# Start addresses of the tiles that TensorE reads as moving operands, and the sums of an RMSNorm by transposition, in a two-layer backbone on one core

## The chip, the cores and the metric

One core of a Trainium2 chip runs the whole program, alone. The metric is the device time of one execution in microseconds (us). A comparison is made of medians over several runs.

## What is computed

The reference runs two layers over 256 context tokens and 256 latent tokens of 1024 features, in float32:

```python
for l in range(DEPTH):                       # 2 layers
    m_lat = split(silu(c) @ w_ada[l] + b_ada[l], 9); m_ctx = the same of c_ctx
    x   = ffn_half(x,   m_lat[0:3], norm_g[l, 0], ffn_w1[l, 0], ffn_w2[l, 0])
    ctx = ffn_half(ctx, m_ctx[0:3], ...)
    h = modulate(rmsnorm(x, norm_g[l, 1]), m_lat[3], m_lat[4]) @ w_in[l]   # and of ctx
    y_lat, y_ctx = token_mixers(...)         # mLSTM, differential, neighbourhood attention
    x = x + m_lat[5] * y_lat
    x = ffn_half(x, m_lat[6:9], norm_g[l, 2], ffn_w1[l, 1], ffn_w2[l, 1])
    if l < DEPTH - 1: the same two steps for ctx
return rmsnorm(x, final_g)
```

`rmsnorm(x)` is `x / sqrt(mean(x*x) + 1e-6) * g`, the mean over the 1024 features of a token; `modulate(h)` is `h * (1 + scale) + shift`; `ffn_half` adds half of a gated `(silu(a) * b) @ w2`.

## The kernel before

All activations lie with features on the partitions and tokens along the free axis: `x` is 8 blocks of [128, 512 tokens], tokens 0 to 255 the context (class 0), 256 to 511 the latents (class 1).

A float32 product is made of three float32r matmuls. Each weight block (`raw`, by DMA) is split by ACT and DVE into `whi` and `wlo` (`weights`, `split`, L217 and L218), and each activation into a high and a low tile: `hhi`/`hlo` for a normed input or for the merged mixers (`split_pair`), `ghi`/`glo` for the gated hidden layer of an FFN (in the very first FFN the low part is two tiles, `head` and `tail`), `ohi`/`olo` for a mixer's output, `st`/`rest` for queries and keys. `three` (L230 to L232) then issues low x whi, high x whi, high x wlo: the weight block of 128x128 stands in the array, and the activation tile is the moving operand, read over 512 columns where both classes are wanted (`slice(0, T)`) or 256 for one class. In `v_part` (L632 to L634) the roles are swapped: a class's h blocks stand, and the weights move, 512 columns each.

The order of PE's instructions is written out by hand. Those of DVE, ACT and POOL are placed by a scheduler in the order of the code and its priorities (`tc.high_priority`). Small pieces of work are put in between the matmuls by `Beside`: a generator is stepped each time a counter of ticks passes given values, and a tick is one call of `three` (or three matmuls of `v_part`).

The norm before each stage is such a generator (`norm_mod`, `rstd_rows`, `rstd_cols`), one for each class. Its steps for a class are: two matmuls of `ssq` (the sums of squares by feature block, [128, 256]) with a column of ones, which leave the sum of each token in a column of PSUM (L260); on DVE the scaling by 1/1024 (L263); on POOL the power -0.5 (L264), giving `r`, [128, 2]; on DVE two diagonal matrices `dg` of it (L274); two matmuls of them with a matrix of ones, which lay the row of factors across all partitions (L278); then for each of 8 feature blocks `u` on DVE (L284), `hhi` on ACT (L286) and `hlo` on DVE (L287). The first step of a norm and its second are given by ticks: `beside.at(gen, (5, 12, 12, 12))` in `norm_begin` and in `ffn`, `(3, 6, 6, 6)` in `mixers`. Class 0's norm runs beside the last matmuls of the stage before, whose last pieces (`end(k)`) take one class, 256 columns, at a time; class 1's norm runs beside class 0's first matmuls of the new stage. The first FFN of the program has a start of its own (`cold_start`), so has the last (`warm_start`), which runs on latents alone, takes its first matmuls on x times the scale, and multiplies by `r` behind them. At the end, `rstd_cols` and a transposition of `x` give the output.

Of the kernel before, what the change touches and what calls it, by code (L numbers as in the profile page):

```python
# [10 lines left out]
F32 = mybir.dt.float32  # L11
F32R = mybir.dt.float32r
AF = mybir.ActivationFunctionType
ALU = mybir.AluOpType
# [97 lines left out]
def tile_backbone(ctx: ExitStack, tc: tile.TileContext, I, out: bass.AP):  # L112
# [27 lines left out]
    ones = cp.tile([P, P], F32, name="ones")  # L140
    nc.gpsimd.memset(ones, 1.0)
    half = cp.tile([P, 8], F32, name="half")
    nc.gpsimd.memset(half, -0.5)

    modT = [cp.tile([P, 9, 2, KC], F32, name=f"modT{l}") for l in range(L)]
# [91 lines left out]
            three(pt[:, at], w, slice(k * P, (k + 1) * P), a, (k0 + k, at), first and k == 0, last and k == n - 1)  # L237
            tick()

    def split_pair(name):  # L240
        return (hp.tile([P, KC, T], F32R, tag="hhi", name="hhi"),
                hp.tile([P, KC, T], F32R, tag="hlo", name="hlo"))


    ssq = cp.tile([P, T], F32, name="ssq")
# [9 lines left out]
    def rstd_cols(cs):  # L255

        n = (cs.stop - cs.start) // P
        p1 = psum()
        for t in range(n):
            mm(p1[:, t:t + 1], ssq[:, cs.start + t * P:cs.start + (t + 1) * P], ones[:, 0:1], start=True, stop=True)  # L260
        r = np_.tile([P, 4], F32, tag="r", name="r")
        with tc.high_priority(offset=AHEAD):
            nc.vector.tensor_scalar(r[:, :n], p1[:, :n], 1.0 / D, EPS, ALU.mult, ALU.add)  # L263
            nc.gpsimd.tensor_tensor(r[:, :n], r[:, :n], half[:, :n], ALU.pow)  # L264
        return r

    def rstd_rows(cs):

        n = (cs.stop - cs.start) // P
        r = rstd_cols(cs)  # L270
        dg = np_.tile([P, 2, P], F32, tag="dg", name="dg", bufs=1)
        with tc.high_priority(offset=AHEAD):
            for t in range(n):
                nc.vector.tensor_scalar_mul(dg[:, t, :], ident, r[:, t:t + 1])  # L274
        yield
        p2 = psum()
        for t in range(n):
            mm(p2[:, t * P:(t + 1) * P], ones, dg[:, t, :], start=True, stop=True)  # L278
        yield p2

    def norm_part(l, which, h, kc, cls, rb):
# [28 lines left out]
    def norm_begin(l, which, h, before):  # L310


        g, g1 = norm_mod(l, which, h, 0), norm_mod(l, which, h, 1)
        beside.at(g, (5, 12, 12, 12))
        for k in range(3):
            before(k)
        beside.drain(g)
        return g1
# [3 lines left out]
    def open_pool(name):  # L322
        e = stack["pool"] = ExitStack()
        return e.enter_context(tc.tile_pool(name=name, bufs=1, reuse_waits="tile"))
# [46 lines left out]
    def ffn(l, i, classes, out_classes_next, before, vectors):  # L371
# [9 lines left out]
        if both and before:  # L381
            gen = norm_begin(l, which, h, before)
        pool = open_pool(f"ff{l}{i}")
        ghi = pool.tile([P, NF, T], F32R, name="ghi")
        junk = pool.tile([P, 512], F32, name="junk") if both else None
        glo = Joined(pool, NF, 6) if cold else pool.tile([P, NF, T], F32R, name="glo")
# [63 lines left out]
        def warm_start():  # L450


            cls = classes[0]
            at = SLICES[1 - cls]
            ws = [w1_unit(k, soon=True, extra=pool if k else None) for k in range(2)]
            sh = pool.tile([P, KC, 32], F32, name="sh")
            nc.gpsimd.memset(sh, 0.0)
            nc.vector.tensor_copy(sh[:, :, 0], modT[l][:, 3 * which, cls, :])
            pts = [psum() for _ in range(2)]
            rows = rstd_rows(cs)  # L460
            for kc in range(KC):
                if kc == WARM[0]:
                    next(rows)
                elif kc == WARM[1]:
                    pr = next(rows)
                    with tc.high_priority(offset=AHEAD):
                        for k in range(KC):
                            norm_part(l, which, h, k, cls, pr[:, 0:256])
                    rb = np_.tile([P, 2, P], F32, tag="dg", name="rb", bufs=1).rearrange("p a t -> p (a t)")
                    nc.scalar.copy(rb, pr[:, 0:256])  # L470
                for pt, w in zip(pts, ws):
                    three(pt[:, cs], w, slice(kc * P, (kc + 1) * P), h, (kc, at), kc == 0, kc == KC - 1)

            pb = psum()
            for kc in range(KC):
                for g in range(4):
                    mm(pb[32 * g:32 * g + 32, 0:P], sh[:, kc, :], ws[g % 2][g // 2][:, kc * P:(kc + 1) * P].bitcast(F32),
                       start=kc == 0, stop=kc == KC - 1)
            lines = np_.tile([P, 256], F32, tag="rows", name="rows", bufs=1)[:, 0:P]
            with tc.high_priority(offset=AHEAD):  # L480
                nc.scalar.copy(lines, pb[:, 0:P])
            yield
            pT = psum()
            nc.tensor.transpose(pT[:, 0:P], lines, ident)
            bias = pool.tile([P, 2], F32, name="bias")
            nc.vector.tensor_reduce(out=bias, in_=pT[:, 0:P].rearrange("p (a m c) -> p m c a", a=2, m=2)[:, :, 0, :],
                                    axis=AX.X, op=ALU.add)
            ab = [pool.tile([P, 256], F32, name=name) for name in ("wa", "wb")]
            for k in range(2):
                nc.vector.tensor_tensor(ab[k], pts[k][:, cs], rb, ALU.mult)  # L490
                nc.scalar.activation(ab[k], ab[k], AF.Identity, bias=bias[:, k:k + 1])
            finish(0, *ab)

        if cold:
            cold_start(FIRST)
        elif not both:
            warm = warm_start()
            next(warm)
        elif both:

            ws = [w1_unit(k, extra=pool if k == 3 else None, soon=k < 2) for k in range(4)]
            pts = [psum() for _ in range(4)]
            beside.at(gen, (5, 12, 12, 12))
            for cls in (0, 1):
                if cls:
                    beside.drain(gen)
                at = SLICES[cls]
                for k in (0, 2):
                    for kc in range(KC):
                        for n in (k, k + 1):  # L510
                            three(pts[n][:, at], ws[n], slice(kc * P, (kc + 1) * P), h, (kc, at), kc == 0, kc == KC - 1)
                            tick()
                    if cls == 1:
                        act(k // 2, pts[k], pts[k + 1])
# [68 lines left out]
    def mixers(l, before):  # L583
# [7 lines left out]
        wf = I["wf"][l]  # L591
        wv = I["wv"][l]
        nlam = late["nlam"]
        h = split_pair("h")
        gen = norm_begin(l, 1, h, before)
        mp = open_pool(f"mx{l}")

# [6 lines left out]
        def loaded(name, shape, src):  # L604
            t = mp.tile(shape, F32, name=name)
            nc.scalar.dma_start(out=t, in_=src)
            return t
# [8 lines left out]
        cb = loaded("cb", [P, 2 * HML], I["conv_b"][l])  # L616
        mg = loaded("mg", [P, 4], I["ml_g"][l])
        dfg = loaded("dfg", [P, 4], I["df_g"][l])

        def proj(tile_i, cs):  # L620
            w = weights(wf[tile_i])
# [111 lines left out]
        pv1 = [psum() for _ in range(NT)]  # L733
        pg = psum()
        wv0, wv1 = weights(wv[0, 0], soon=True), weights(wv[0, 1], soon=True)
        beside.at(gen, (3, 6, 6, 6))
        wg = gate_weights()
        v_part(pv1, wv0, 0, (0, 1))
        v_part(pv1, wv1, 1, (0, 1))
# [416 lines left out]
        oT = [out_pair()]  # L1156
        na_out(oT[0])
        tgs.append(gate(2, 7, "t2k"))
        y = split_pair("y")
        for d2 in range(4):  # L1160
            branch(2, d2, oT[0], tgs[2 * d2:2 * d2 + 2], y)
        beside.drain()
# [192 lines left out]
```

## Time and profile before

| | us |
|---|---|
| median of 3 runs (lowest to highest) | 2288.07 (2287.82 to 2288.58) |
| the profiled execution, its own time | 2288.0 |
| its span, from the first instruction to the last | 2286.2 |
| busy: PE, its weight loads, DVE, ACT, POOL | 2253.8, 1948.1, 1580.5, 935.5, 81.3 |
| bytes read from HBM, over the span | 312.3 MB, 137 GB/s |

Two names are of use in reading it. The profile gives a matmul a start and a duration; the durations overlap, since one matmul enters the array while the one before it leaves, so what a stream of matmuls costs is read from one start to the next, not from the durations. And a matmul of float32 operands (not float32r) is shown as two records, a transposition as one: the two matmuls of L260 in a norm are four records.

### The profile page before, as it was taken

What the parts mean: (1) busy time and instruction counts of PE and PEld (TensorE: products, weight loads), DVE (VectorE), ACT (ScalarE), POOL (GpSimd) and SP (SyncE); (2) the same over time, 40 slices, a digit from 0 to 9 for tenths busy, and PEclk for the clock granted to TensorE, in tenths of its full rate; (3) what the DMA queues carried; (4) which work ended last, traced back from release to release, by engine and by line L of the source; (5) the groups of instructions that cost most, each with busy time, mean ns of one, the idle gap of its engine ahead of it and who ended that gap; (6) DMA issues with size and microseconds to landing.
All of it is one profiled execution on the core that took longest, in us unless ns stands there. A gap on an engine that the chain in (4) does not pass through costs nothing.

```text
span 2286.2 us, 33657 instructions
## 1 busy us (share of the span) xinstructions
PE 2253.8 (99%) x12845; PEld 1948.1 (85%) x12845; DVE 1580.5 (69%) x3398; ACT 935.5 (41%) x1687; POOL 81.3 (4%) x137
## 2 busy tenths in 40 slices
PE   7999999999999999999999999999999999999998
PEld 5888889888888788898888898888898898899998
DVE  5989944887665564676665479898248885768654
ACT  4323222455654553332322232322234675556443
POOL 0000000001002110000000000000000001200000
PEclk9999999999999999999999999999999999999999
DMA  8556543312222322334444436566323243445554
GB/s 302 179 199 203 192 136 97 102 65 74 74 84 85 92 83 83 111 116 147 161 151 144 138 111 205 201 202 197 100 95 115 70 137 122 138 145 169 184 178 136
DMA packets 94034, 315.55 MB, mean 138 GB/s; under 512 B 12928, under 2 KB 13712, under 8 KB 93872
## 3 DMA queue, kind: packets, MB, share of 16 engines
q1 hardware_dynamic: 89072, 308.07, 41.1%
q0 software_dynamic: 2144, 4.36, 1.4%
q8 instruction: 101, 1.65, 0.3%
q10 hardware_dynamic: 2656, 0.96, 0.2%
q14 instruction: 61, 0.50, 0.1%
HBM read 312.30 MB, written 1.05 MB: 137 GB/s over the span
## 4 chain that ended last, share of the span: by engine, by line
PE 87%; issue 9%; DVE 2%; DMA 1%; ACT 1%; POOL 0%; SPq 0%; POOLq 0%; DVEq 0%; ACTq 0%
PE p L230 25%; PE p L232 24%; PE p L231 24%; PE p L632 2%; PE p L634 2%; PE p L633 2%; PE p L657 1%; PE p L897 1%; PE p L1104 1%; DMA room<-in_w_ada 1%; PE p L952 1%; PE p L951 1%; PE p L1022 1%; PE p L874 1%; DVE wlo L218 0%
## 5 line engine op out<-in xcount | busy, mean ns | idle before, releaser
L230 PE MATMUL p<-hlo,whi 128*128 128x512 f32 (+1 forms) x2424 | 864.3, 357 | 2.7 <-DVE hlo L287 2.7
L232 PE MATMUL p<-hhi,wlo 128*128 128x512 f32 (+1 forms) x2424 | 848.5, 350 | 0.0
L231 PE MATMUL p<-hhi,whi 128*128 128x512 f32 (+1 forms) x2424 | 848.5, 350 | 0.0
L217 ACT CAST whi<-raw 128x1024 fp32r<-128x1024 f32 (+1 forms) x436 | 451.2, 1035 | 872.2 <-PE p L231 773.7
L218 DVE TENSOR_TENSOR wlo<-raw,whi 128x1024 fp32r<-128x1024 f32 (+1 forms) x436 | 524.0, 1202 | 292.2 <-ACT whi L217 291.2
L230 PEld LDWEIGHTS p<-hlo,whi 128*128 128x128 f32 x2424 | 459.8, 190 | 64.5 <-issue 3.7
L232 PEld LDWEIGHTS p<-hhi,wlo 128*128 128x128 f32 x2424 | 459.6, 190 | 59.8
L231 PEld LDWEIGHTS p<-hhi,whi 128*128 128x128 f32 x2424 | 459.9, 190 | 58.4 <-issue 1.9
L232 PE MATMUL p<-ghi,wlo 128*128 128x256 f32 (+1 forms) x836 | 278.2, 333 | 0.0
L231 PE MATMUL p<-ghi,whi 128*128 128x256 f32 (+1 forms) x836 | 276.7, 331 | 0.0
L196 DVE SCALAR_TENSOR_TENSOR junk<-raw,scb 128x512 f32<-128x512 f32 x256 | 176.1, 688 | 96.0 <-DMA raw<-in_w_adaT 95.5
L230 PE MATMUL p<-glo,whi 128*128 128x256 f32 (+1 forms) x616 | 203.1, 330 | 1.2 <-DVE x L305 1.2
L196 DVE SCALAR_TENSOR_TENSOR raw<-raw,scb 128x512 f32<-128x512 f32 x256 | 176.7, 690 | 6.1
L232 PEld LDWEIGHTS p<-ghi,wlo 128*128 128x128 f32 x836 | 156.9, 188 | 17.4
L231 PEld LDWEIGHTS p<-ghi,whi 128*128 128x128 f32 x836 | 156.8, 188 | 16.8
L230 PEld LDWEIGHTS p<-glo,whi 128*128 128x128 f32 x616 | 115.8, 188 | 11.5 <-DVE x L305 1.6
L305 DVE SCALAR_TENSOR_TENSOR x<-p,gmod,x 128x256 f32<-128x256 f32 x80 | 36.5, 480 | 83.6 <-PE p L232 83.3
L632 PE MATMUL p<-wlo,hhi 128*128 128x512 f32 x192 | 76.1, 396 | 0.0
L634 PE MATMUL p<-whi,hlo 128*128 128x512 f32 x192 | 74.9, 390 | 0.0
L633 PE MATMUL p<-whi,hhi 128*128 128x512 f32 x192 | 74.8, 390 | 0.0
L217 ACT CAST ghi<-g 128x512 fp32r<-128x512 f32 (+1 forms) x88 | 49.9, 567 | 58.2 <-DVE g L392 57.9
L230 PE MATMUL p<-olo,whi 128*128 128x512 f32 (+1 forms) x192 | 68.3, 356 | 0.0
(242 smaller groups left out, 2392.1 us busy)
## 6 DMA issues: line engine op xcount, KB each, us to landing
raw<-in_w SPq DMA_DIRECT2D x208, 512.0 KB, 3.4
raw<-in_w_adaT SPq DMA_DIRECT2D x128, 512.0 KB, 3.5
raw<-in_wf SPq DMA_DIRECT2D x106, 512.0 KB, 3.3
raw<-in_w SPq DMA_DIRECT2D x64, 448.0 KB, 3.3
raw<-in_wv SPq DMA_DIRECT2D x24, 512.0 KB, 3.2
raw<-in_wb SPq DMA_DIRECT2D x24, 512.0 KB, 3.3
room<-in_w_ada SPq DMA_DIRECT2D x16, 512.0 KB, 11.1
raw<-in_wo SPq DMA_DIRECT2D x16, 512.0 KB, 3.3
```

The lines of the kernel that those rows point to most:

```text
L196: nc.vector.scalar_tensor_tensor(w if cls else junk, w, 1.0, scb[:, cls, :], ALU.mult, ALU.mult, accum_out=acc[:, kc, i, cls:cls + 1])
L217: nc.scalar.copy(hi, src)
L218: nc.vector.tensor_sub(lo, src, hi.bitcast(F32))
L230: mm(dst, w[0][:, wat], a[1][:, aat[0], aat[1]], start=start, stop=False)
L231: mm(dst, w[0][:, wat], a[0][:, aat[0], aat[1]], start=False, stop=False)
L232: mm(dst, w[1][:, wat], a[0][:, aat[0], aat[1]], start=False, stop=stop)
L305: nc.vector.scalar_tensor_tensor(x[:, dt, cs], pt[:, cs], gmod[l][:, which, cls, dt:dt + 1], x[:, dt, cs], ALU.mult, ALU.add)
L632: mm(pts[t], h[0][:, kc, at], w[1][:, wat], start=kc == 0, stop=False)
L633: mm(pts[t], h[0][:, kc, at], w[0][:, wat], start=False, stop=False)
L634: mm(pts[t], h[1][:, kc, at], w[0][:, wat], start=False, stop=kc == KC - 1)
L657: nc.tensor.transpose(pt[:, k * P:(k + 1) * P], a, ident)
L874: mm(pS[:, rs], k[:, at], q[:, rs], start=True, stop=True)
```

## The change

It has three parts.

1. Padding is put ahead of some tiles (in `np_`, in the pools of the last FFN and of the mixers, and inside `hhi`/`hlo`, which become 32 elements longer), so that their start addresses in a partition move. The matmuls and their order stay. The table gives, for the float32r moving operands, the start address modulo 128 bytes in the two built programs; a read of class 1 starts 1024 bytes behind the tile's start, so it has the same remainder.

| moving tile | columns | reads | before | after |
|---|---|---|---|---|
| ghi, glo, head, tail | 512 | 1188 | 64 | 0 |
| ghi, glo, head, tail (FFNs of both classes) | 256 | 792 | 64 | 0 |
| ghi, glo (last FFN) | 256 | 528 | 64 | 64 |
| hhi, hlo | 512 | 4344 | 0 | 0 |
| hhi, hlo (layer 1's mixers, keys) | 512 | 288 | 0 | 64 |
| hhi, hlo (layer 1's mixers, last FFN) | 256 | 2240 | 0 | 64 |
| hhi, hlo (elsewhere) | 256 | 560 | 0 | 0 |
| ohi, olo | 512 | 288 | 32 | 0 |
| ohi, olo | 256 | 288 | 32 | 64 |
| st, rest (layer 0; layer 1) | 512 | 64; 64 | 32 | 0; 64 |
| st, rest | 256 | 64 | 32 | 0 |
| whi, wlo (as moving operands) | 512 | 576 | 0 | 0 |

2. The two matmuls with ones that sum `ssq` become two transpositions, and DVE sums the 128 columns of each (`tensor_reduce` over [128, 2, 128] in PSUM) ahead of the scaling. The two diagonal matrices and their matmuls become two transpositions of `r`, each column of it broadcast over 128 columns; the `dg` work on DVE is gone.

3. The ticks of a norm's second step go from 12 to 14 in the FFNs and at the end of each stage, and from 6 to 7 in the mixers.

```diff
-    def split_pair(name):
-        return (hp.tile([P, KC, T], F32R, tag="hhi", name="hhi"),
-                hp.tile([P, KC, T], F32R, tag="hlo", name="hlo"))
+    def split_pair(name, half_line=False):
+
+        at = 16 if half_line else 0
+        got = (hp.tile([P, KC * T + 32], F32R, tag="hhi", name="hhi"),
+               hp.tile([P, KC * T + 32], F32R, tag="hlo", name="hlo"))
+        return tuple(t[:, at:at + KC * T].rearrange("p (k t) -> p k t", k=KC) for t in got)
...
         for t in range(n):
-            mm(p1[:, t:t + 1], ssq[:, cs.start + t * P:cs.start + (t + 1) * P], ones[:, 0:1], start=True, stop=True)
+            nc.tensor.transpose(p1[:, t * P:(t + 1) * P], ssq[:, cs.start + t * P:cs.start + (t + 1) * P], ident)
         r = np_.tile([P, 4], F32, tag="r", name="r")
         with tc.high_priority(offset=AHEAD):
-            nc.vector.tensor_scalar(r[:, :n], p1[:, :n], 1.0 / D, EPS, ALU.mult, ALU.add)
+            nc.vector.tensor_reduce(out=r[:, :n], in_=p1[:, 0:n * P].rearrange("p (t c) -> p t c", t=n),
+                                    axis=AX.X, op=ALU.add)
+            nc.vector.tensor_scalar(r[:, :n], r[:, :n], 1.0 / D, EPS, ALU.mult, ALU.add)
             nc.gpsimd.tensor_tensor(r[:, :n], r[:, :n], half[:, :n], ALU.pow)
...
         r = rstd_cols(cs)
-        dg = np_.tile([P, 2, P], F32, tag="dg", name="dg", bufs=1)
-        with tc.high_priority(offset=AHEAD):
-            for t in range(n):
-                nc.vector.tensor_scalar_mul(dg[:, t, :], ident, r[:, t:t + 1])
         yield
         p2 = psum()
         for t in range(n):
-            mm(p2[:, t * P:(t + 1) * P], ones, dg[:, t, :], start=True, stop=True)
+            nc.tensor.transpose(p2[:, t * P:(t + 1) * P], r[:, t:t + 1].to_broadcast([P, P]), ident)
         yield p2
...
-        beside.at(g, (5, 12, 12, 12))
+        beside.at(g, (5, 14, 14, 14))
...
+        if not both:
+            pool.tile([P, 16], F32, name="half_line")
...
-        h = split_pair("h")
+        h = split_pair("h", not full)
...
+        mp.tile([P, 8 if full else 24], F32, name="line")
...
-        beside.at(gen, (3, 6, 6, 6))
+        beside.at(gen, (3, 7, 7, 7))
...
-        y = split_pair("y")
+        y = split_pair("y", not full)
```

Three places show how it moves instructions (line numbers of the changed kernel are a few higher). The first is PE at the end of layer 0's mixers, where class 0's norm for the next FFN lies between the matmuls of w_out. Before:

```order
L278 MATMUL p<-dg,ones 128x128 x2
L230 MATMUL p<-hlo,whi 128x256
L231 MATMUL p<-hhi,whi 128x256
L232 MATMUL p<-hhi,wlo 128x256
L230 MATMUL p<-hlo,whi 128x256
L231 MATMUL p<-hhi,whi 128x256
L232 MATMUL p<-hhi,wlo 128x256
```

and with the change, over the same stretch:

```order
L231 MATMUL p<-hlo,whi 128x256
L232 MATMUL p<-hhi,whi 128x256
L233 MATMUL p<-hhi,wlo 128x256
L231 MATMUL p<-hlo,whi 128x256
L232 MATMUL p<-hhi,whi 128x256
L233 MATMUL p<-hhi,wlo 128x256
L280 MATMUL p<-c_ident,r 128x128 x2
```

The second step of the norm stands two calls of `three` later, and is two transpositions (moving operand `c_ident`, the unit matrix).

The second place is DVE in the same norm (`x` is the residual sum of a block, `ssq` the running sum of squares, `wlo` the split of a weight block). Before:

```order
L263 TENSOR_SCALAR r<-p 128x2
L274 TENSOR_SCALAR dg<-c_ident,r 128x128 x2
L305 SCALAR_TENSOR_TENSOR x<-p,gmod_97,x 128x256
L218 TENSOR_TENSOR wlo<-raw,whi 128x1024
L284 SCALAR_TENSOR_TENSOR u<-x,amod_95,p 128x256 x3
L305 SCALAR_TENSOR_TENSOR x<-p,gmod_97,x 128x256
L253 TENSOR_TENSOR ssq<-ssq,sq 128x256
L218 TENSOR_TENSOR wlo<-raw,whi 128x1024
L253 TENSOR_TENSOR ssq<-ssq,sq 128x256
L305 SCALAR_TENSOR_TENSOR x<-p,gmod_97,x 128x256
L218 TENSOR_TENSOR wlo<-raw,whi 128x1024
L287 SCALAR_TENSOR_TENSOR hlo<-u,modT_93,hhi 128x256 x2
```

With the change:

```order
L267 TENSOR_REDUCE r<-p 128x2
L269 TENSOR_SCALAR r<-r 128x2
L307 SCALAR_TENSOR_TENSOR x<-p,gmod_98,x 128x256
L219 TENSOR_TENSOR wlo<-raw,whi 128x1024
L257 TENSOR_TENSOR ssq<-ssq,sq 128x256
L286 SCALAR_TENSOR_TENSOR u<-x,amod_96,p 128x256 x3
L307 SCALAR_TENSOR_TENSOR x<-p,gmod_98,x 128x256
L219 TENSOR_TENSOR wlo<-raw,whi 128x1024
L257 TENSOR_TENSOR ssq<-ssq,sq 128x256
L307 SCALAR_TENSOR_TENSOR x<-p,gmod_98,x 128x256
L219 TENSOR_TENSOR wlo<-raw,whi 128x1024
L289 SCALAR_TENSOR_TENSOR hlo<-u,modT_94,hhi 128x256 x2
```

The two `dg` rows are gone, a reduction is new, and the `ssq` of a block, which needs ACT's square of it, stands ahead of the three `u` instead of behind them.

The third place is DVE in class 1's norm at the start of layer 0's mixers. `mg` and `dfg` are small constants that come by DMA from ACT's queue, `nselr` the copy of another, `wg` the split of the gates' weights. Before:

```order
L274 TENSOR_SCALAR dg<-c_ident,r 128x128 x2
L287 SCALAR_TENSOR_TENSOR hlo<-u,modT_93,hhi 128x256 x2
L218 TENSOR_TENSOR wg<-raw,wg 128x8x8 x2
L284 SCALAR_TENSOR_TENSOR u<-x,amod_95,p 128x256 x3
L287 SCALAR_TENSOR_TENSOR hlo<-u,modT_93,hhi 128x256 x2
L284 SCALAR_TENSOR_TENSOR u<-x,amod_95,p 128x256
L287 SCALAR_TENSOR_TENSOR hlo<-u,modT_93,hhi 128x256
L284 SCALAR_TENSOR_TENSOR u<-x,amod_95,p 128x256 x2
L287 SCALAR_TENSOR_TENSOR hlo<-u,modT_93,hhi 128x256
L748 CAST nselr<-nsel 128x64
L814 TENSOR_SCALAR mg<-mg 128x4
```

With the change:

```order
L267 TENSOR_REDUCE r<-p 128x2
L289 SCALAR_TENSOR_TENSOR hlo<-u,modT_94,hhi 128x256
L269 TENSOR_SCALAR r<-r 128x2
L289 SCALAR_TENSOR_TENSOR hlo<-u,modT_94,hhi 128x256
L219 TENSOR_TENSOR wg<-raw,wg 128x8x8 x2
L286 SCALAR_TENSOR_TENSOR u<-x,amod_96,p 128x256 x3
L289 SCALAR_TENSOR_TENSOR hlo<-u,modT_94,hhi 128x256
L819 TENSOR_SCALAR mg<-mg 128x4
L820 TENSOR_SCALAR dfg<-dfg 128x4
L286 SCALAR_TENSOR_TENSOR u<-x,amod_96,p 128x256
L289 SCALAR_TENSOR_TENSOR hlo<-u,modT_94,hhi 128x256 x2
L286 SCALAR_TENSOR_TENSOR u<-x,amod_96,p 128x256
```

`mg` and `dfg` now stand behind the first `hlo` of class 1 instead of behind the fourth and the seventh, and `nselr` further back. The queue of ACT issues the same DMAs in the same order. Layer 1's mixers change alike.

## Rows read from the trace of the kernel before

**Rows 1.** The page, busy time: engine, busy us (share of the span), instructions.

```profile
PE 2253.8 (99%) x12845; PEld 1948.1 (85%) x12845; DVE 1580.5 (69%) x3398; ACT 935.5 (41%) x1687; POOL 81.3 (4%) x137
```

**Rows 2.** The page, costliest groups: busy us, mean ns, idle before and its releaser.

```profile
L217 ACT CAST whi<-raw 128x1024 fp32r<-128x1024 f32 (+1 forms) x436 | 451.2, 1035 | 872.2 <-PE p L231 773.7
```

**Rows 3.** Timeline of PE, 100 to 140 us: start us, duration us, instruction.

```profile
99.83 0.39 PE L230 MATMUL p<-hlo,whi 128*128 128x512 f32 x1
...
139.95 0.39 PE L230 MATMUL p<-hlo,whi 128*128 128x512 f32 x1
```

**Rows 4.** Timeline of PE, 310 to 350 us.

```profile
309.61 0.39 PE L230 MATMUL p<-head,whi 128*128 128x512 f32 x1
...
349.44 0.39 PE L230 MATMUL p<-tail,whi 128*128 128x512 f32 x1
```

**Rows 5.** Timeline of PE, 902 to 922 us.

```profile
902.13 0.39 PE L230 MATMUL p<-olo,whi 128*128 128x512 f32 x1
...
921.81 0.39 PE L230 MATMUL p<-olo,whi 128*128 128x512 f32 x1
```

**Rows 6.** Timeline of PE, 2100 to 2122 us.

```profile
2099.95 0.28 PE L230 MATMUL p<-hlo,whi 128*128 128x256 f32 x1
...
2121.91 0.28 PE L230 MATMUL p<-hlo,whi 128*128 128x256 f32 x1
```

**Rows 7.** Timeline of PE, 2220 to 2242 us.

```profile
2219.73 0.28 PE L230 MATMUL p<-glo,whi 128*128 128x256 f32 x1
...
2241.99 0.28 PE L230 MATMUL p<-glo,whi 128*128 128x256 f32 x1
```

**Rows 8.** Timeline of PE, 389.5 to 391 us.

```profile
389.98 0.28 PE L232 MATMUL p<-ghi,wlo 128*128 128x256 f32 x1
390.09 0.50 PE L260 MATMUL p<-ones,ssq 128*128 128x1 f32 x4
...
390.66 0.28 PE L231 MATMUL p<-ghi,whi 128*128 128x256 f32 x1
```

**Rows 9.** Timeline of PE, 600 to 601.5 us.

```profile
600.29 0.39 PE L232 MATMUL p<-hhi,wlo 128*128 128x512 f32 x1
600.52 0.38 PE L657 MATMUL p<-c_ident,de 128*128 128x128 f32 x2
...
600.98 0.40 PE L231 MATMUL p<-hhi,whi 128*128 128x512 f32 x1
...
601.45 0.40 PE L230 MATMUL p<-hlo,whi 128*128 128x512 f32 x1
```

**Rows 10.** Timeline of PE, 966 to 974 us.

```profile
968.53 0.28 PE L232 MATMUL p<-hhi,wlo 128*128 128x256 f32 x1
971.49 0.58 PE L230 MATMUL p<-hlo,whi 128*128 128x256 f32 x1 [2.67 <-DVE hlo L287]
```

**Rows 11.** Timeline of ACT, 960 to 985 us.

```profile
968.74 1.04 ACT L217 CAST whi<-raw 128x1024 fp32r<-128x1024 f32 x1 [1.51 <-PE p L231]
```

**Rows 12.** Stretches: busy us (instructions) of each engine, granted PE clock, DMA share, GB/s.

```profile
971.50:977.60 6.10, 6.10 (x28) 6.04 (x28) 3.67 (x12) 1.52 (x3) 0.70 (x1) 0.50 0.25 86
```

**Rows 13.** Timeline of ACT and its queue (ACTq), 392 to 420 us.

```profile
404.01 0.44 ACTq L606 DMA_DIRECT2D dfg<-in_df_g  x1
...
406.19 0.33 ACTq L606 DMA_DIRECT2D nsel<-in_nsel  x1
```

**Rows 14.** Timeline of DVE, 392 to 420 us.

```profile
406.06 0.88 DVE L287 SCALAR_TENSOR_TENSOR hlo<-u,modT,hhi 128x256 fp32r<-128x256 f32 x2
...
409.33 0.20 DVE L748 CAST nselr<-nsel 128x64 fp32r<-128x64 f32 x1 [0.43 <-DMA nsel<-in_nsel]
...
413.24 0.48 DVE L287 SCALAR_TENSOR_TENSOR hlo<-u,modT,hhi 128x256 fp32r<-128x256 f32 x1
```

**Rows 15.** Timeline of PE, 413 to 416 us.

```profile
415.16 0.28 PE L728 MATMUL p<-hlo,wg 128*128 128x256 f32 x1
```

**Rows 16.** Groups by form, DVE: the same columns as rows 2.

```profile
L1078 DVE TENSOR_REDUCE nmx<-p 128x1 f32<-128x256 f32 x16 | 6.2, 415 | 6.7 <-PE p L952 6.7
```

More of the change, by code (lines that the diff above doesn't have):

```diff
@@ L142, in tile_backbone @@
     half = cp.tile([P, 8], F32, name="half")
+    np_.tile([P, 16], F32, tag="line", name="line", bufs=1)
     nc.gpsimd.memset(half, -0.5)
@@ L468, in warm_start @@
                             norm_part(l, which, h, k, cls, pr[:, 0:256])
-                    rb = np_.tile([P, 2, P], F32, tag="dg", name="rb", bufs=1).rearrange("p a t -> p (a t)")
+                    rb = np_.tile([P, 256], F32, tag="dg", name="rb", bufs=1)
                     nc.scalar.copy(rb, pr[:, 0:256])
@@ L502, in ffn @@
             pts = [psum() for _ in range(4)]
-            beside.at(gen, (5, 12, 12, 12))
+            beside.at(gen, (5, 14, 14, 14))
             for cls in (0, 1):
```

## The prediction

> **What bounds the kernel now.** I read the busy times first: PE is busy for 99% of the span [rows 1], and the reader is to see that no other engine comes near. Then the groups: ACT's cast of a weight block, the head of the chain that feeds PE, sits idle for 872 us, 774 of them waiting for PE to give a weight buffer back [rows 2]. So weights are ready ahead of PE, and what PE saves on its own stream comes off the end, stage by stage, except where PE itself waits. Last I read PE's timeline, from start to start, since durations of matmuls overlap.
>
> That timeline, laid beside the start addresses of the change's table, shows three spacings for 512 columns. In the first FFN, hhi and hlo start at 0 modulo 128 bytes: 177 steps take 139.95 - 99.83 = 40.12 us, 226.7 ns each [rows 3]. head, tail and ghi start at 64: 174 steps in 39.83 us, 228.9 ns [rows 4]. olo and ohi start at 32: 84 steps in 19.68 us, 234.3 ns [rows 5]. For 256 columns the order turns round: at 0, 183 steps in 21.96 us, 120.0 ns [rows 6]; at 64, 189 steps in 22.26 us, 117.8 ns [rows 7]. All five stretches run without a gap. They differ in tiles and stages too, so the address is inferred; but tiles of other pools with the same remainder keep the same spacing (whi and wlo moving in the v products that of rows 3, glo in the later FFNs that of rows 4).
>
> **The addresses, term by term** (reads of the change's table times the difference of these spacings).
> - 512 columns from 64 to 0, 1188 reads x 2.24 ns: -2.7 us.
> - 512 columns from 32 to 0, 288 of ohi and olo and 64 of st and rest, x 7.6 ns: -2.7.
> - 512 columns from 32 to 64, 64 reads x 5.4: -0.3.
> - 512 columns from 0 to 64 (layer 1's keys), 288 x 2.24: +0.6.
> - 256 columns from 0 to 64, 2240 x 2.22: -5.0.
> - 256 columns from 64 to 0 (the FFNs of both classes, whose tiles serve both widths), 792 x 2.22: +1.8.
> - 256 columns from 32 to 64 or 0: no clean stretch shows them; between 117.8 and 120.0 on either side, 352 reads come to 0.8 us at most one way or the other, and I take 0.
>
> Sum -8.3 us. Bounds: if the address is not the cause, 0. On the other side, the reads of hhi and hlo at 0 are not always at 227 ns: behind a group of float32 matmuls they stand at 235, as the two steps from 600.98 to 601.45 do [rows 9]. I count 744 of the 4344 between 228 and 240 ns, most in layer 0's mixers. If they fell into step once no neighbour starts at 32, that would be 744 x 6 ns, a further -4.4. I take none of it, since the stretch of rows 9 comes from a transposition and not from a 32.
>
> **The norms on PE.** A pair of float32 matmuls is four records. From the matmul ahead of them to the second behind them is 390.66 - 389.98 = 0.68 us [rows 8]; without them it would be two spacings, 0.24, so the group costs 0.44. Two transpositions cost 600.98 - 600.29 = 0.69 less two spacings of 0.227, so 0.24 [rows 9]. A group that turns from the one into the other saves 0.21 us. There are 12 sums and 11 row spreads; without the cold start's four, where PE waits for weights anyway, and the last sum, which ends the program, 18 lie in PE's stream: -3.8 us.
>
> **The norms' chain.** On DVE the two dg products go, and with them a wait for POOL inside DVE's order; a reduction of 256 columns comes in, 415 ns by the attention's own [rows 16]. In the middle of the program the chain has room. The second step stands two ticks later, six matmuls of 0.12 us or 0.7 us, less 0.42 that PE saves by then, so the factors come 0.3 us later relative to PE (0.26 in the mixers, with one tick of 0.68). The shortest room I find where PE does not already wait is that of the last block of class 1 in the mixers: written by 413.24 + 0.48 = 413.72 [rows 14], read at 415.16 [rows 15], 1.4 us. It covers that. Cost 0; if the cover were gone, each tenth lost is a tenth of PE's.
>
> The moved mg and dfg are a new wait. nsel was usable 3.1 us after its issue (406.19 to 409.33) [rows 13, 14], so dfg, issued at 404.01, is usable at 407.1. DVE comes to it behind the first hlo of class 1, of the pair that begins at 406.06 [rows 14], so at about 406.5, and waits 0.6 us. Queued behind it are the other blocks' u and hlo, which PE needs in turn, and they have the 1.4 us or more. Cost 0, twice in the program.
>
> At the end nothing hides the chain: the reduction adds 0.4 us, PE's shorter sum gives 0.2 back: +0.2.
>
> **Where PE waits now.** At the start of layer 0's second FFN PE stops from 968.53 to 971.49 for the first hlo [rows 10]. ACT could make hhi only behind a cast that waits for the weight buffer which PE's last matmul gives back, at 968.74 [rows 11]; ACT's order there is not changed, and the whole wait moves with PE. Behind it PE's granted clock is 0.50, the 1.2 GHz level, for 6.1 us in which it is busy all the time [rows 12], so some 3 us are lost. I keep both. Late next, should a stall go, would be the third weight block's split.
>
> **Sum**: -8.3 - 3.8 + 0.2 = -11.9 us. The profiled execution took 2288.0, the median of the runs is 2288.07, the same; so 2276.1.
>
> **A rule against the change.** The rows say that 512 columns cost 226.7, 228.9 or 234.3 ns by where they start [rows 3 to 5]. The Trainium skill, "SBUF — State Buffer", in its specifications and its note on cachelines, has lines of 16 bytes and a penalty for leaving a line too early: starts at 0, 32 and 64 all begin a line and read the same number of whole lines, so by it the padding would give nothing. No run here shows lines of 16 bytes, and rows 3 to 7 speak against that being all there is.
>
> **Rivals.**
> 1. The address does not count; the spacings belong to the stages (their DMA traffic, their PSUM use) and stay. For it: no tile is read at two addresses with the same width in this trace. Against: one remainder, one spacing, across stages. It leaves -3.8 + 0.2: 2284.4, less than 0.2% from before. This is also what the page's rule comes to.
> 2. Only one width follows the address. 512 columns alone give -2.7 - 2.7 - 0.3 + 0.6 = -5.1, with the norms 2279.3; 256 alone give -5.0 + 1.8 = -3.2, so 2281.2.
> 3. More than the sum: the float32r reads of the mixers fall into step (-4.4, 2271.7), or the 0.50 stretch at 971 us does not come, since PE arrives there a few us earlier (-3, 2273.1); both, 2268.7.
> 4. Slower: a norm comes late. If class 0's first hlo missed PE at the start of both mixers and of layer 1's first FFN as it does at 971 us, each place would cost the wait of 2.67 and the half clock's 3.05 [rows 10, 12], 5.7 us, and three of them 17.1: 2288.0 - 11.9 + 17.1 = 2293.2. It decides where the factors come later than the room: over 1.4 us against the 0.3 (0.9 with the DMA) worked out above. ACT's order speaks for it a little, since in both mixers two casts now stand ahead of the first hhi.
>
> **How the numbers follow.** The sum, 2276.1, with a range of its own of 2273.5 to 2279.0, I give 0.68; rival 3 0.14; rival 2 0.08; rival 1 0.06; rival 4 0.04. About 0.2% (4.6 us) is what a measurement of this kernel can tell from no change. Faster by more: 0.68 + 0.14 + 0.08 = 0.90; within it 0.06; slower 0.04. The range leaves out rivals 1 and 4 and the ends of 2 and 3: 2269.5 to 2281.0.
>
> **What would show it.** In the profile after, 512 columns of ghi should stand at 226.7 ns and not 228.9, those of ohi near 227, and the last FFN's 256 columns of hhi at 117.8 and not 120.0, while 256 columns of ghi in FFNs of both classes rise to 120. A norm's two groups should each take 0.24 us and be two records. The wait of some 2.7 us at the start of layer 0's second FFN should stand where it did, with a half-clock stretch behind it. The prediction is wrong if those spacings stay as they are, or if PE shows new waits for hlo in the mixers.

## The result, and the profile after

The changed kernel takes **2303.0 us** (median of 4 runs, 2301.1 to 2304.2), the kernel before beside it 2287.95 (2286.4 to 2288.6): a ratio of 1.0065, 95% interval 1.0053 to 1.0076. It is **slower by 15 us, where 2276.1 was forecast**. The profiled execution took 2301.13 us, its span 2299.4, against 2288.0 and 2286.2.

The page's busy times and its group of the weight casts (busy us, mean ns, idle before and its releaser), to be laid beside [rows 1, 2]:

```profile
PE 2266.4 (99%) x12799; PEld 1935.7 (84%) x12799; DVE 1581.5 (69%) x3388; ACT 936.1 (41%) x1687; POOL 82.2 (4%) x137
L218 ACT CAST whi<-raw 128x1024 fp32r<-128x1024 f32 (+1 forms) x436 | 451.0, 1035 | 925.8 <-PE p L232 829.2
```

PE is still busy for 99% of the span, with 46 records fewer and 12.6 us more. The cast waits longer for PE than before. So weights do not come too late: PE's own stream has become slower.

The timeline of PE (start us, duration us, instruction), four stretches that answer to [rows 3 to 6]:

```profile
99.08 0.40 PE L231 MATMUL p<-hlo,whi 128*128 128x512 f32 x1
...
139.68 0.40 PE L231 MATMUL p<-hlo,whi 128*128 128x512 f32 x1
...
316.08 0.40 PE L231 MATMUL p<-tail,whi 128*128 128x512 f32 x1
...
349.68 0.40 PE L231 MATMUL p<-tail,whi 128*128 128x512 f32 x1
...
911.06 0.39 PE L231 MATMUL p<-olo,whi 128*128 128x512 f32 x1
...
929.43 0.39 PE L231 MATMUL p<-olo,whi 128*128 128x512 f32 x1
...
2108.76 0.28 PE L231 MATMUL p<-hlo,whi 128*128 128x256 f32 x1
...
2131.86 0.28 PE L231 MATMUL p<-hlo,whi 128*128 128x256 f32 x1
```

- hhi and hlo with 512 columns, whose remainder modulo 128 did not change: 174 steps in 40.60 us, **233.3 ns, for 226.7 before** [rows 3].
- tail and ghi, moved from 64 to 0: 144 steps in 33.60 us, **233.3 ns, for 228.9** [rows 4], where 226.7 was forecast.
- olo and ohi: 81 steps in 18.37 us, 226.8 ns, for 234.3 [rows 5], as forecast.
- hhi and hlo with 256 columns: 196 steps in 23.10 us, 117.9 ns, for 120.0 [rows 6], as forecast (one of the 196 is a transposition in between).

Two of the four go the wrong way, and they are the wide ones: 4632 and 1188 reads. The built program tells what they have in common. hhi starts where it did, but is 128 bytes longer, so hlo, the next tile, starts 128 bytes further on. Modulo 128 that is nothing. The tiles behind the two start 320 bytes further on: twice 128, and 64 for the padding in `np_`. **Modulo 256, hlo went from 0 to 128, and ghi, glo, head and tail from 64 to 128**; ohi and olo are at 0 (layer 0). In the kernel before, every tile that I had called "0" was at 0 modulo 256 as well.

Adding up PE's timeline from each start to the next by kind of instruction, against the profiled execution of before, gives the account below; the other columns are kernels of the next section. A wait of PE is counted with the instruction ahead of it. The cold start lies in two rows and nearly cancels: about -1.3 in the norms', +1.6 in the rest.

| us against before | the change | hlo mended (`e2`) | and g at 0 (`e5`) | layer 1's h at 112 (`e8`) |
|---|---|---|---|---|
| hhi, hlo, 512 columns, 4632 reads | +17.6 | +0.2 | -0.8 | -0.3 |
| ghi, glo, head, tail, 512 columns, 1188 | +4.5 | +5.2 | -2.7 | -2.7 |
| v products (whi, wlo moving), 576 | +3.3 | +2.8 | +2.7 | +2.8 |
| ohi, olo, 512 columns, 288 | -1.2 | -1.4 | -1.3 | -1.3 |
| 256 columns of h, g and o, 4408 | -6.6 | -4.7 | -6.0 | -12.1 |
| the norms' sums and row spreads | -6.4 | -6.3 | -6.7 | -6.4 |
| the rest (start, end, other matmuls) | +1.9 | +2.4 | +1.9 | +2.1 |
| sum | +13.1 | -1.8 | -12.9 | -17.9 |

The first row is less than 4632 times the 6.6 ns of the first FFN: over the 960 such reads of layer 0's second FFN the change stands at 231.1 ns, not 233.3 (226.7 before). Why the two differ is not shown.

### The profile page after: what moved, and what is told of

The parts are those of the page before. It is cut to its first block, busy times and chain, and to the rows that moved or that the text cites. A ratio compares the mean times of both kernels' runs of the same rounds, so it can differ in the third digit from the quotient of the medians.

```text
span 2299.4 us, 33562 instructions
## 1 busy us (share of the span) xinstructions
PE 2266.4 (99%) x12799; PEld 1935.7 (84%) x12799; DVE 1581.5 (69%) x3388; ACT 936.1 (41%) x1687; POOL 82.2 (4%) x137
## 4 chain that ended last, share of the span: by engine, by line
PE 86%; issue 9%; DVE 3%; DMA 1%; ACT 1%; SPq 0%; POOLq 0%; POOL 0%; DVEq 0%; ACTq 0%
PE p L231 25%; PE p L233 24%; PE p L232 24%; PE p L639 2%; PE p L638 2%; PE p L637 2%; PE p L662 1%; PE p L902 1%; PE p L1109 1%; DMA room<-in_w_ada 1%; PE p L957 1%; PE p L956 1%; PE p L1027 1%; PE p L879 1%; DVE wlo L219 1%
## 5 line engine op out<-in xcount | busy, mean ns | idle before, releaser
L233 PEld LDWEIGHTS p<-ghi,wlo 128*128 128x128 f32 x836 | 158.1, 189 | 17.6
L396 DVE TENSOR_TENSOR g<-g,p 128x512 f32<-128x512 f32 (+1 forms) x87 | 54.0, 621 | 29.9 <-PE p L233 29.4
```

The costliest lines, as they stand in the source:

```text
L233: mm(dst, w[1][:, wat], a[0][:, aat[0], aat[1]], start=False, stop=stop)
L396: nc.vector.tensor_tensor(g, g, b, ALU.mult)
```

## The experiments

After the result I held three theories. **A**: what counts is the moving tile's own start, but modulo 256. **B**: it is the distance between the start of the moving and that of the standing tile, or of the low and the high tile, which here looks like A because whi and wlo start at 0 modulo 256 nearly everywhere. **C**: the addresses have nothing to do with it, and the new norms or something at the start put the stream into another state.

**Mend one length.** `e2_line256`: the change, with hhi and hlo 64 elements longer in place of 32.

```diff
-        got = (hp.tile([P, KC * T + 32], F32R, tag="hhi", name="hhi"),
-               hp.tile([P, KC * T + 32], F32R, tag="hlo", name="hlo"))
+        got = (hp.tile([P, KC * T + 64], F32R, tag="hhi", name="hhi"),
+               hp.tile([P, KC * T + 64], F32R, tag="hlo", name="hlo"))
```

> The changed kernel with hhi and hlo 64 elements longer instead of 32, so that hlo starts at 0 (or 64) modulo 256 as hhi does, not at 128 (192); all other remainders stay. Theories A and B: hlo and hhi back at 226.7 ns, the v products too, so 17.6 and 3.3 us come off: 2303.0 - 20.9 = about 2282. Theory C: 2303.

Measured: 2283.8 us (10 runs), ratio 0.9985 (0.9975 to 0.9994). The same stretch of PE's timeline as above:

```profile
98.98 0.39 PE L231 MATMUL p<-hlo,whi 128*128 128x512 f32 x1
...
139.78 0.39 PE L231 MATMUL p<-hlo,whi 128*128 128x512 f32 x1
```

180 steps in 40.80 us, 226.7 ns again. 128 bytes in one tile's length are worth 19 us. C falls. The v products did not come back as expected (+2.8 in the account); `e5_g0` below shows why.

**One part of the change each.** `e3_norms` is the kernel before with the transpositions, the reduction and the new ticks; `e4_addr` is the change's padding with the norms and ticks of before.

```diff
# e3_norms, against the kernel before
-            mm(p1[:, t:t + 1], ssq[:, cs.start + t * P:cs.start + (t + 1) * P], ones[:, 0:1], start=True, stop=True)
+            nc.tensor.transpose(p1[:, t * P:(t + 1) * P], ssq[:, cs.start + t * P:cs.start + (t + 1) * P], ident)
...
# e4_addr, against the changed kernel
-            nc.tensor.transpose(p1[:, t * P:(t + 1) * P], ssq[:, cs.start + t * P:cs.start + (t + 1) * P], ident)
+            mm(p1[:, t:t + 1], ssq[:, cs.start + t * P:cs.start + (t + 1) * P], ones[:, 0:1], start=True, stop=True)
...
```

> The kernel before with the new norms and ticks alone, no address moved. Theories A and B: the norm groups' saving alone, 4 to 6 us: 2282 to 2284. Theory C, if the transpositions put the stream out of step: 2300 or more.

> The changed kernel with the norms and ticks of the kernel before: the addresses alone. Theories A and B: the changed kernel's time plus the norms' 4 to 6 us: 2307 to 2309. Theory C: about the kernel before, 2288.

Measured: the norms alone 2284.09 us, ratio 0.9985 (0.9975 to 0.9994), 3.4 us below the 2287.44 beside it. The padding alone 2307.06, ratio 1.0086 (1.0071 to 1.0101), 19.6 us above. The two parts are nearly additive: 19.6 - 3.4 = 16.2, for the 15 of the whole. The norms were forecast right, the padding with the wrong sign.

**The starts by themselves.** `e1_starts` runs triples (low moving tile over high standing, high over high, high over low), 16 in a row, at each pair of starts, at both widths.

```python
for w in STAND:            # standing tiles wa..wd start at 0, 64, 128, 192
    for m in MOVE:         # moving tiles la..lh (low), ha..hh (high) at 0, 32, ... 224
        seg512(m, w)
```

> This kernel leaves the whole network out: it runs streams of float32r triples (low x first block, high x first block, high x second block) alone, 48 matmuls for each pair of start addresses, and gives zeros and one block of PSUM back. The moving tiles start at 0, 32, ... 224 bytes past a multiple of 1024 (la/ha to lh/hh), the standing ones at 0, 64, 128, 192 (wa/va to wd/vd). Theory A (the moving operand's start modulo 256 bytes sets the spacing): 512 columns from 0 at 226.7 ns, from 64 and 192 at 229, from 32, 96, 160, 224 at 234, from 128 at 232 to 235, the same whatever the standing start is. Theory B (what counts is where moving and standing operands, or low and high tile, start relative to each other): moving 128 beside standing 128 is as fast as 0 beside 0, and equal low and high tiles are faster than low at 128 with high at 0. Theory C (not the addresses, but a state of the stream that something before it leaves behind): one spacing for all starts, and other values where the same starts come a second time.

Of its trace, by line and tile, the first matmul of each triple: duration ns min/median/max, first and last start us. From the first to the last are 15 triples.

```profile
L67 PE MATMUL p<-la,wa x16: 389/389/389, 26.9 to 37.1; 128*128 128x512 f32 x16
...
L67 PE MATMUL p<-lc,wa x16: 388/388/398, 49.0 to 59.3; 128*128 128x512 f32 x16
...
L67 PE MATMUL p<-le,wa x16: 392/394/398, 71.2 to 81.7; 128*128 128x512 f32 x16
...
L67 PE MATMUL p<-la,wb x16: 394/394/399, 116.0 to 126.5; 128*128 128x512 f32 x16
...
L67 PE MATMUL p<-lc,wb x16: 389/389/395, 138.4 to 148.7; 128*128 128x512 f32 x16
...
L67 PE MATMUL p<-le,wb x16: 388/388/398, 160.5 to 170.9; 128*128 128x512 f32 x16
```

10.2 us for (0, 0) and 10.5 for (128, 0), the start that hlo got. But (0, 64) takes 10.5 too, and (64, 64) 10.3: the start of 0 is slow once the standing tile is elsewhere. In ns a triple from the single starts, moving start across, standing start down:

| 512 columns | 0 | 64 | 128 | 192 | | 256 columns | 0 | 64 | 128 | 192 |
|---|---|---|---|---|---|---|---|---|---|---|
| 0 | 680 | 687 | 700 | 700 | | 0 | 359 | 354 | 356 | 353 |
| 64 | 700 | 682 | 687 | 700 | | 64 | 341 | 360 | 354 | 356 |
| 128 | 700 | 700 | 682 | 687 | | 128 | 356 | 341 | 360 | 354 |
| 192 | 687 | 700 | 700 | 680 | | 192 | 340 | 356 | 353 | 360 |

At 512 columns each diagonal holds one value: 680 to 682 at a distance of 0, 687 where the moving tile stands 64 past the standing one, 700 otherwise (the odd 32s lie at 699 to 703). The distance of low from high tile can't be all of it, since the two are equal in every cell. **A falls; B stands, as the distance modulo 256 of moving from standing tile.** At 256 columns a distance of 0 is the slowest of the four, 360, and three pairs show a value that had not stood out in any trace so far, 340.

The low tile alone at 128 with a high one at 0, the very case of hhi and hlo, gave 699.5 ns here, as much as when all three matmuls are at 128, and as the changed kernel's 3 x 233.3 in its first FFN. The reverse, low at 0 and high at 128, gave only 686.5, though two of its three matmuls are at 128. So where distances are mixed the cost is not a price for each read, and the rule is shown for triples that share one distance. Behind four transpositions the starts 0, 64, 128 and 192 settled at 680, 687, about 697 and 700: the order does not change.

**Put g back too.** `e5_g0`: `e2` with hlo's own tail shortened, which moves all tiles behind it by 128, and the mixers' padding lengthened to keep ohi where it is.

```diff
-                hp.tile([P, KC * T + 64], F32R, tag="hlo", name="hlo"))
+                hp.tile([P, KC * T + 32], F32R, tag="hlo", name="hlo"))
...
-        mp.tile([P, 8 if full else 24], F32, name="line")
+        mp.tile([P, 40 if full else 56], F32, name="line")
```

> The changed kernel with the low tile's length mended (both h tiles start at 0 modulo 256 or, in layer 1's mixer and the last FFN, at 64) and, new here, ghi, glo, head and tail moved from 128 to 0 modulo 256 (64 in the last FFN); ohi and olo stay where the changed kernel has them. From the run with the mended h tiles, 2283.8 us: 1188 reads of 512 columns come back from about 700 ns a triple to 680, 7.2 us; some 750 reads of 256 columns go from 118.7 to 119.9 ns, +0.9. Theories A (the moving tile's own start modulo 256) and B (its distance modulo 256 from the standing tile, which is at 0 nearly everywhere): 2277.5 us. Theory C (no addresses): 2283.8.

Measured: **2275.43 us**, ratio 0.9947 (0.9931 to 0.9964). This is the kernel that the prediction described, the wide reads of h, g and o at 0 (layer 1's keys at 64) and layer 1's narrow ones at 64, and it takes what was predicted, 2276.1.

It also shows the standing tile at work inside the kernel. In the v products whi and wlo are the moving operands, at 0 throughout; hhi and hlo stand, at 0 in layer 0 and at 64 in layer 1. PE's timeline of one such stretch in each layer:

```profile
434.92 0.39 PE L637 MATMUL p<-wlo,hhi 128*128 128x512 f32 x1
...
456.45 0.39 PE L639 MATMUL p<-whi,hlo 128*128 128x512 f32 x1
...
1731.84 0.39 PE L637 MATMUL p<-wlo,hhi 128*128 128x512 f32 x1
...
1754.01 0.39 PE L639 MATMUL p<-whi,hlo 128*128 128x512 f32 x1
```

95 steps each: 21.53 us, 226.6 ns, and 22.17 us, 233.4 ns. In the kernel before, where hhi and hlo stand at 0 in both layers, the second one is as fast as the first, 21.54 us:

```profile
1740.31 0.39 PE L632 MATMUL p<-wlo,hhi 128*128 128x512 f32 x1
...
1761.85 0.39 PE L634 MATMUL p<-whi,hlo 128*128 128x512 f32 x1
```

Over layer 1's 288 of them that comes to some 1.7 us of the account's +2.7. The other 1.0 is no address: `e3_norms`, which moves none, has it too (+1.0). It is a new wait, once in each mixer, for the last sum of squares of class 1. DVE, then PE, in layer 0, before:

```profile
401.06 0.42 DVE L253 TENSOR_TENSOR ssq<-ssq,sq 128x256 f32<-128x256 f32 x1
```

```profile
401.33 0.40 PE L634 MATMUL p<-whi,hlo 128*128 128x512 f32 x1
401.63 0.58 PE L260 MATMUL p<-ones,ssq 128*128 128x1 f32 x4
```

and with the change:

```profile
408.15 0.42 DVE L257 TENSOR_TENSOR ssq<-ssq,sq 128x256 f32<-128x256 f32 x1
```

```profile
407.94 0.40 PE L639 MATMUL p<-whi,hlo 128*128 128x512 f32 x1
408.71 0.41 PE L264 MATMUL p<-c_ident,ssq 128*128 128x128 f32 x2 [0.37 <-DVE ssq L257]
```

The step into the sum takes 0.77 us for 0.30; layer 1 is alike (0.75 for 0.27).

**Shift everything.** `e7_shift`: `e5` and 64 bytes ahead of all work tiles. All starts move, no distance does.

```diff
     half = cp.tile([P, 8], F32, name="half")
+    cp.tile([P, 16], F32, name="shift")
```

> The run with h and g tiles at 0 modulo 256 (2275.4 us), and one more tile of 64 bytes ahead of all work tiles, which moves moving and standing tiles together: weights to 64 modulo 256, tiles read by 512 columns to 64, those of layer 1's mixer and the last FFN to 128; the distances stay. Theory A (the moving tile's own start): about 5,900 reads of 512 columns go from 226.7 to 229.1 ns, +14 us, those of 256 columns cost about the same in sum, 2289 us. Theory B (the distance from the standing tile): nothing changes, 2275.4 us.

Measured: 2278.17 us (2276.5 to 2279.9), ratio 0.996 (0.9946 to 0.9974). The first FFN, with hhi, hlo, whi and wlo all at 64:

```profile
98.71 0.39 PE L232 MATMUL p<-hlo,whi 128*128 128x512 f32 x1
...
139.51 0.39 PE L232 MATMUL p<-hlo,whi 128*128 128x512 f32 x1
```

180 steps in 40.80 us, 226.7 ns: a start of 64 is as good as 0 when both have it. A's 2289 is out. B's 2275.4 is 2.8 us off, but the interval overlaps that of `e5`. In the profiled executions the span is 1.3 us longer, and that is the 340s: counted from each matmul with 256 columns at a distance of 64, three steps last 340 ns in 365 of 2890 cases in `e5` and in 61 here, 304 x 4.4 ns = 1.3 us.

**Where the 340 comes from.** `e6_hist` runs the 256-column pairs in four orders.

> A second program of triples alone (it computes nothing of the reference; its output is zeros): 256-column triples for moving starts 0, 64, 128, 192 against standing starts 0, 64, 128, 192, in four orders and behind four transpositions, then moving starts 16, 48, ... 240 against 0 at both widths, then triples whose low standing tile starts elsewhere than the high one. In the first such program 512 columns took 680 ns a triple whenever moving and standing start were equal modulo 256 and 687 to 703 otherwise, which refutes A and bears out B. For 256 columns it gave 353 to 360, but 340 for (0,64), (64,128) and (0,192). B1: that is a property of the pair, so the same three pairs give 340 in every order and all others 353 to 360. B2: it is one of two patterns that a stream can fall into at a distance of 64 or 192, and depends on what ran before, so other pairs give 340 and these three 353 in some orders. For the last part: if a matmul's spacing goes by the start of the standing tile that is loaded beside it for the next matmul, a low standing tile at 64 slows the second matmul of a triple; if by its own, the third.

Moving 192 over standing 0, in the first and the second order of its timeline:

```profile
97.51 0.28 PE L69 MATMUL p<-ld,wa 128*128 128x256 f32 x1
...
102.81 0.28 PE L69 MATMUL p<-ld,wa 128*128 128x256 f32 x1
...
143.23 0.29 PE L77 MATMUL p<-ld,wa 128*128 128x256 f32 x1
...
148.35 0.28 PE L77 MATMUL p<-ld,wa 128*128 128x256 f32 x1
```

45 steps in 5.30 us and in 5.12. In the first all triples take 352 to 354 ns, in the second 358, 341 and then 340 to the end. Same tiles, same code, another predecessor: B2. A distance of 64 or 192 has both patterns, and each holds once it is there; 0 and 128 never showed 340. The last part, low and high standing tile at different starts, gave 689 to 701 ns a triple with the loss spread over two or three of its matmuls, so whether a matmul goes by its own standing tile or by the one loaded beside it **stays open**. Among the eight odd starts 112 reached 340, after four triples.

**Use it.** `e8_112` puts layer 1's h tile at 112 in place of 64; `e9_g112` also the last FFN's ghi and glo.

```diff
# e8_112
-        at = 16 if half_line else 0
+        at = 28 if half_line else 0
...
# e9_g112 (a tile of the last FFN; both of ghi and glo, in place of the padding ahead of them)
+            t = pool.tile([P, NF * T + 64], F32R, name=name)
+            return t[:, 28:28 + NF * T].rearrange("p (k t) -> p k t", k=NF)
```

> The run with h and g tiles at 0 modulo 256 (2275.4 us), with layer 1's h tile at 112 past it in place of 64, because 256-column triples settled at 340 ns there in the second program of triples. 2217 reads of 256 columns: if they settle at 340 ns a triple, 113.3 for 117.8 ns, -9.8 us, 2266 us; if they stay at a pattern of 353 to 360, 2275 to 2280 us. Theory B2 (which pattern a stream falls into depends on what ran before) expects a mixture, about 2271; A has nothing to say on it but 2275.

> The run with layer 1's h tile at a distance of 112 (2270.1 us), with the last FFN's ghi and glo, 528 reads of 256 columns, moved from 64 to 112 as well. If they settle at 340 ns a triple as five in six of the h reads did, 117.8 to about 114.5 ns, -1.8 us: 2268.3 us; if they stay at 353, 2270.1.

Measured: `e8_112` **2270.08 us, ratio 0.9921 (0.9907 to 0.9936)**; `e9_g112` 2268.44, ratio 0.9914 (0.9901 to 0.9928), which can't be told from it. Both beat the kernel before and the changed one. hlo and hhi in the last FFN of `e8_112`:

```profile
2089.85 0.28 PE L231 MATMUL p<-hlo,whi 128*128 128x256 f32 x1
...
2110.93 0.28 PE L231 MATMUL p<-hlo,whi 128*128 128x256 f32 x1
```

186 steps in 21.08 us, 113.3 ns, for the 120.0 of [rows 6]. At a distance of 112, three steps last 340 ns in 1759 of 2123 cases.

**A finer grid.** `e10_grid`: moving starts 0, 16, ... 240 against 0, in four orders.

> A third program of triples alone (it computes nothing of the reference; its output is zeros): moving starts 0, 16, ... 240 against standing 0, 256 columns in three orders and behind four transpositions, 512 columns in a fourth order. B2 expects 112 to settle at 340 ns in most of the four, 64 and 192 in some, 0 and 128 in none; at 512 columns 680 at 0 alone, 687 at 64 and 690 to 705 elsewhere.

Its first two orders and the one behind transpositions, moving start 0 (la) and 112 (lh), the first matmul of each triple:

```profile
L69 PE MATMUL p<-la,wa x16: 277/283/283, 34.2 to 39.6; 128*128 128x256 f32 x16
...
L69 PE MATMUL p<-lh,wa x16: 275/275/275, 74.1 to 79.2; 128*128 128x256 f32 x16
...
L77 PE MATMUL p<-lh,wa x16: 275/275/282, 169.9 to 175.1; 128*128 128x256 f32 x16
...
L96 PE MATMUL p<-lh,wa x16: 275/275/367, 336.6 to 341.9; 128*128 128x256 f32 x16
```

112 settled at 340 in all four orders, here after none to four triples (behind the transpositions the first one takes 443); 192 did in all four, 64 in none this time, 0 and 128 never. At 512 columns 0 gave 680, 64 687, all other starts 693 to 710.

## Why the prediction was wrong, point by point

**The step that failed** is in the first part: "tiles of other pools with the same remainder keep the same spacing", with the table's remainder modulo 128 bytes. The spacing did follow an address, as argued, but by the wrong measure, twice over: modulo 256, not 128, and as a distance from the standing tile. The trace of before could not tell these apart, since whi and wlo stood at 0 nearly everywhere and its moving tiles at 0, 64 and 160 modulo 256, never at 128. So the sum has no term for the 4344 reads of hhi and hlo that are "0" before and after. A third of them, hlo's, changed their distance to 128, and the whole triple slowed: with layer 1's keys +17.6 us. ghi, glo, head and tail, priced at 0 and built at 128, add +4.5 for the -2.7 forecast. The built program held the needed number, a tile 128 bytes longer and its neighbour 128 bytes on; it was reduced to a remainder before it was looked at.

Term by term:

- *512 columns from 64 to 0, -2.7 us.* Real when the tiles are really at 0: -2.7 in `e5_g0`. In the changed kernel they are at 128: +4.5.
- *512 columns from 32 to 0, -2.7, and 32 to 64, -0.3.* ohi and olo -1.2 for the 2.2 of theirs; right in sign, half the size: the 96 reads of [rows 5] gain their 7.5 ns, the 192 between other matmuls less than 3. st and rest gained nothing (+0.3).
- *Layer 1's keys from 0 to 64, +0.6.* They took some 0.3 to 0.4. The v products, where the same tile stands, had no term: of the +2.7 in `e5_g0` some 1.7, since standing at 64 puts the moving whi and wlo at a distance of 192 (233.4 ns for 226.7, above).
- *256 columns, -5.0 and +1.8.* In `e5_g0`, -5.3 for layer 1's h and +1.4 for g, with 365 cases of 340 ns that nobody forecast (365 x 4.4 ns, 1.6 us, a part of it ohi's and olo's). The rest of the account's -6.0 is mostly the clock at layer 0's second FFN, below.
- *The norms, -3.8, and the end, +0.2.* Right for the groups, and in sum: a group is two records and takes 0.46 us less two spacings of 0.12, 0.22 us, for the 0.24 forecast and the 0.44 of before [rows 8, 9]; `e3_norms` is 3.4 us faster. PE's timeline around one sum:

```profile
396.99 0.28 PE L233 MATMUL p<-ghi,wlo 128*128 128x256 f32 x1
397.11 0.38 PE L264 MATMUL p<-c_ident,ssq 128*128 128x128 f32 x2
397.25 0.36 PE L231 MATMUL p<-head,whi 128*128 128x256 f32 x1
397.45 0.27 PE L232 MATMUL p<-ghi,whi 128*128 128x256 f32 x1
```

- *The norms' chain, cost 0.* Wrong, by about 1 us. The room that was looked for was that of hlo; the sum of class 1 had less. Before, its ssq is written by 401.06 + 0.42 = 401.48 and PE's sum starts at 401.63; with the change DVE writes it later against PE, and PE waits in both mixers (shown above). Whether the later ticks or the new order of DVE does it was not tried apart. PE's waits for ssq, in total, times and longest, before and after:

```profile
PE p L260 <- DVE ssq L253: 1.0, 1, 1.0
```

```profile
PE p L264 <- DVE ssq L257: 2.1, 4, 1.1
```

- *The new wait of mg and dfg, 0.* Right: dfg's DMA goes out at 410.57 and DVE uses it at 413.83 with no wait shown. ACT's queue, then DVE:

```profile
410.57 0.44 ACTq L610 DMA_DIRECT2D dfg<-in_df_g  x1
```

```profile
413.76 0.16 DVE L819 TENSOR_SCALAR mg<-mg 128x4 f32<-128x4 f32 x1
413.83 0.16 DVE L820 TENSOR_SCALAR dfg<-dfg 128x4 f32<-128x4 f32 x1
```

- *Rival 4, a late norm.* It gave the right sign and was not the cause: no new wait for hlo appears in the mixers, those for ssq cost about 1 us, and `e5_g0`, with the same norms and ticks, is fast.
- *The wait at layer 0's second FFN.* It stays, 2.95 us from start to start as before [rows 10]. The half clock behind it does not, in this execution. PE's timeline, then the stretch behind the wait (us, busy of each engine, granted PE clock, DMA share, GB/s):

```profile
977.64 0.27 PE L233 MATMUL p<-hhi,wlo 128*128 128x256 f32 x1
980.59 0.39 PE L231 MATMUL p<-hlo,whi 128*128 128x256 f32 x1 [2.68 <-DVE hlo L289]
```

```profile
980.60:988.00 7.40, 7.09 (x56) 6.79 (x57) 7.37 (x21) 2.78 (x6) 0.86 (x1) 1.00 0.23 71
```

The granted clock is 1.00, for the 0.50 of [rows 12], and that, not an address, is some 2 us of the account's -6.6 for 256 columns. The 3 us that the prediction put on the half clock are too many: from the first h matmul behind the wait to the hundredth it is 15.12 us in `e9_g112`, at 0.56, and 13.17 in `e5_g0`, at 1.00, with the same order and the same addresses there. The changed kernel is slower in spite of it.

- *Rival 1 and the cacheline rule.* The padding alone made the kernel 19.6 us slower, and 112 in place of 64 took about 5 us off; starts are not free. The Trainium skill, "SBUF — State Buffer", in its note on cachelines, has lines of 16 bytes. By that alone all starts tried here would be alike, since each is a multiple of 16; the runs do not agree.

`e5_g0` lands within 1 us of 2276.1, but partly by luck. The forecast had no term for the +2.7 of the v products and the new wait, and gained too much from ohi, st and rest. It also had none for the 1.6 of the 340s and some 2 of the clock (in the profiled execution), and these made up for it.

## What to carry to other kernels

A remainder that fits all rows of one trace is a fit, not a law: before pricing a move by it, list the full start addresses of moving and standing tiles, before and after, and ask which coarser modulus or which difference of the two would fit as well. Padding a tile moves every tile behind it, so print the neighbours' addresses too; and a small program of the bare matmul stream over a grid of starts costs one run and settles what a full kernel cannot. Here it then paid 17.6 us (2270.08 for the 2287.71 beside it), 3.4 of them the norms': wide reads at a distance of 0 from the weights, layer 1's narrow ones at 112.

## What was not expected

- The spacing of float32r matmuls in triples that share one distance follows that distance, between moving and standing tile, modulo 256 bytes: at 512 columns 226.7 ns at 0, 229 at 64, 230 to 237 elsewhere. Why it does is not shown.
- The best distance for 512 columns, 0, is at the slow end for 256 (120.0 ns); 112 gives 113.3 in most of the stream.
- At 256 columns a stream can hold one of two patterns at the same addresses, 353 or 340 ns a triple, by what ran before it.
- The half-clock stretch behind the same 2.95 us gap came in four of the nine profiled executions of the full kernel (granted clock 0.50 in [rows 12]; over the 7 us behind it 0.76 in `e2_line256` and `e3_norms` and 0.56 in `e9_g112`) and not in five (1.00). What decides it was not tried.
